# Five edits to the order of loads, splits and products in a conformer, attention and SwiGLU block

## The chip, the cores and the metric

The kernel runs on one core of a Trainium2 chip. The metric is the device time in microseconds (us) of one execution, and the median over several runs is compared. The engines are named as in the profile: PE (the matrix engine, with PEld for its weight loads), DVE (VectorE), ACT (ScalarE), POOL (GpSimd) and SP (SyncE, which only issues transfers). A letter q behind an engine's name (ACTq) marks a DMA issue on that engine's queue.

## What is computed

One block on x of 1024 x 1024 with a conditioning vector c: a token mixer with a convolution branch and an attention branch, merged by sigmoid gates, and a SwiGLU feed-forward part, each between two RMS norms with scale, shift and gate from c.

```python
mod = silu(c) @ ada_w + ada_b
sh1, sc1, ga1, sh2, sc2, ga2 = split(mod, 6)
h = rmsnorm(x, pre_mix_g) * (1 + sc1) + sh1
proj = h @ w_in
glu_in, qkv, gates = split(proj, [1024, 2560])
u = u_val * sigmoid(u_gate)                       # u_val, u_gate = halves of glu_in
u = silu(layernorm(causal_depthwise_conv(u), conv_ln_g, conv_ln_b))
y_conv = u @ w_conv_out                           # 512 -> 1024
y_att = stick_breaking_attention(qkv) @ w_att_out # 512 -> 1024
g_conv, g_att = split(gates, 2)
y = (sigmoid(g_conv) * y_conv + sigmoid(g_att) * y_att) @ w_o
x = x + ga1 * rmsnorm(y, post_mix_g)
h = rmsnorm(x, pre_ffn_g) * (1 + sc2) + sh2
gate, up = split(h @ w_ffn_in, 2)                 # 1024 -> 2 x 2816
y = (silu(gate) * up) @ w_ffn_out
out = x + ga2 * rmsnorm(y, post_ffn_g)
```

All of it is float32.

## The kernel before, in words

Every large product is made of three matmuls: an operand is split into a high part, rounded to the fast format fp32r by an ACT copy (`copy_to`, L145), and a low part, the rest, by a DVE subtraction. The product is high x high, high x low and low x high (in the tables `w[0]` is the high part, `w[1]` the low one). The gates, the feed-forward input and the feed-forward output are besides computed by a scheme of Strassen's kind: of 2 x 2 blocks, seven products instead of eight, whose operands (T1 to T4, s1 to s4) are sums of blocks made on DVE. One product is 12 matmuls of 128 x 512 and fills one PSUM bank.

The stages that the change touches, in order of time:

- **Plain gates and early products, 405 to 466 us.** Two of the 16 gate tiles (`PLAIN`, L617 to L623) are computed directly: ACT makes `sg` by a sigmoid, and `store` (L101) writes it to DRAM from POOL's queue. Then, for seven pairs of gate tiles, `early(i, q)` makes two of the seven products ahead, each into bank `k_i`, which ACT evacuates into `ee` (L635) and stores from its own queue (L636) into `e_d` for q = 0 and `s_d` for q = 1. The `sg` and `ee` tiles share two slots; the `k` banks rotate over three PSUM banks.
- **Gate pairs, layer norm, projection, 466 to 590 us.** `other_five(i)` makes the other five products of a pair; after one of the pairs, `ln_all` does the layer norm of the convolution branch (`cr`, `la`, `lm`; its split outputs are `hhi`, `hlo`, `cb`). `y_conv(n)` then multiplies them by the projection weight `wc` (products `pyc`, L747). `load_w` takes one tile from each of three rotating slot groups: raw, high and low. The high and low slots are the same that the gate pairs' operands (`w_op`) use.
- **Early feed-forward products, 741 to 850 us.** `ke(f, i)` (L1102) makes two of the seven products for feed-forward tiles ahead of the rounds, and `e(f, i)` evacuates them; `wh` and `wlo` make the weight's two parts. `t12`, `t3`, `t4`, `hi_of` and `lo_of` make the operands T1 to T4. `r0` and `r1` are generators: each `next` writes the next step of feed-forward round 0 or 1 (`ffn`, L1372) into the program. This section is written by hand in the order in which it is to run, and `pin` fixes that order on PE, DVE and ACT.
- **Sweep 1, from 1170 us.** `prep1(j, w)` (L1604) splits the weights (`wa11`, `wa12`, through `wop2`, whose slots alternate between the groups `whi` and `wlo`) and the feed-forward's inner activations (`gb11`, `gb21`, through `op2`).

Outside the pinned section a scheduler sorts the instructions of each engine, from the order in which they are written and from priorities; within an engine they then run in that order. A transfer is issued by the engine whose `dma_start` is called, in that engine's order: `load` by SP, `store` by POOL.

## Time and profile before

| | |
|---|---|
| median of 3 runs | 1400.02 us (1399.16 to 1400.69) |
| profiled execution | 1400.8 us, span of its records 1399.0 us |
| granted clock of PE, mean | 0.994 |
| busy share of the span | PE 98%, PEld 82%, DVE 75%, ACT 47%, POOL 8% |
| matmuls | 6778 |

How to read the rows: a timeline row has the start in us from the span's start, the duration, the engine, the line of the kernel, the operation, what it writes and reads, the shape, how many were merged into the row (x), and in brackets the idle time of the engine before it with what ended that idleness. Matmuls overlap, so a row of one has 0.39 us although the next starts 0.23 us later. A row of the waits has the engine, the line, what was waited for, and then us in total, times, longest.

### The profile page before, as it was taken

The page shows a single profiled execution, that of the slowest core. Times are in us where ns is not written, and L with a number is a line of the kernel's source. Part 1 is how long each engine was busy: PE and PEld are TensorE (multiplying, and loading weights), DVE is VectorE, ACT ScalarE, POOL GpSimd, SP SyncE. Part 2 cuts the span into 40 slices and gives each one's busy share as a digit, 9 for nine tenths or more (in the row PEclk, how much of TensorE's full clock was granted, in tenths as well). Part 3 has the DMA queues.
Part 4 walks back from the last instruction along what each step waited for, and adds up shares of the span by engine and source line. Part 5 has one row for each costly group of instructions (what it writes and reads, how often), then busy time and mean ns, then how long its engine had stood idle before and what let it go on. Part 6 is the DMA issues. An engine that isn't in the chain of part 4 may idle for free.

```text
span 1399.0 us, 18714 instructions
## 1 busy us (share of the span) xinstructions
PE 1370.6 (98%) x6778; PEld 1150.3 (82%) x6778; DVE 1043.6 (75%) x1592; ACT 651.5 (47%) x1147; POOL 109.4 (8%) x251
## 2 busy tenths in 40 slices
PE   8999999999999999999999999999999999999996
PEld 5898898998987887888887778888888887888886
DVE  7898586775858789677597887778887876785355
ACT  6375465464546456213366553334454444433441
POOL 0100000000000011000012100001111110000002
PEclk8999999999999999999999999999999999999999
DMA  9512050141359646855845635457777779586736
GB/s 384 204 31 76 31 166 31 61 121 46 123 191 318 203 128 233 308 183 176 311 136 188 196 115 192 142 179 249 252 241 263 248 240 398 176 330 229 249 110 121
DMA packets 94684, 265.01 MB, mean 189 GB/s; under 512 B 10048, under 2 KB 21440, under 8 KB 93568
## 3 DMA queue, kind: packets, MB, share of 16 engines
q1 hardware_dynamic: 74352, 201.68, 43.2%
q0 software_dynamic: 18224, 58.47, 11.9%
q10 hardware_dynamic: 2016, 3.67, 0.7%
q8 instruction: 53, 0.87, 0.3%
q14 instruction: 39, 0.32, 0.1%
HBM read 192.74 MB, written 71.04 MB: 189 GB/s over the span
## 4 chain that ended last, share of the span: by engine, by line
PE 76%; issue 14%; DVE 3%; DMA 3%; ACT 2%; POOL 1%; POOLq 0%; DVEq 0%; SPq 0%; ACTq 0%
PE ka L1001 14%; PE ka L1543 9%; PE kc L1001 8%; PE pwo L919 5%; PE pb L1543 4%; PE pgv L166 3%; PE pyc L747 3%; PE pya L166 3%; PE pv L478 3%; PE pq L166 2%; PE pk L166 2%; PE pgg L166 2%; PE pa L1543 2%; PE kb L1001 2%; PE tr L574 2%
## 5 line engine op out<-in xcount | busy, mean ns | idle before, releaser
L550 ACT ACTIVATE ka<-z 128x128 f32<-128x128 f32 (+2 forms) x96 | 47.4, 496 | 53.0 <-PE z L549 43.7
L556 DVE TENSOR_TENSOR_SCAN ka<-ka,eye 128x128 f32<-128x128 f32 (+1 forms) x64 | 51.9, 824 | 17.1 <-ACT ka L550 17.1
L1543 PE MATMUL ka<-gt,w2f 128*128 128x512 f32 x264 | 63.4, 389 | 0.0
L121 DVE SCALAR_TENSOR_TENSOR ada<-ada,cb 128x1024 f32<-128x1024 f32 x32 | 39.0, 1223 | 27.5 <-DMA ada<-in_ada_dram 27.5
L1543 PEld LDWEIGHTS ka<-gt,w2f 128*128 128x128 f32 x264 | 49.6, 188 | 10.3
L561 DVE TENSOR_TENSOR be<-be,ka 128x127 f32<-128x127 f32 (+2 forms) x96 | 52.0, 553 | 7.2 <-ACT be L552 1.8
L1109 PE MATMUL ke<-b,w_hi 128*128 128x512 f32 x176 | 55.2, 395 | 0.0
L552 ACT ACTIVATE be<-z 128x127 f32<-128x127 f32 (+2 forms) x96 | 47.0, 496 | 3.9 <-PE tr L574 3.8
L574 PE MATMUL tr<-ident,be 128*128 128x128 f32 x288 | 47.3, 272 | 0.0
L559 DVE TENSOR_TENSOR_SCAN ka<-ka 128x512 f32<-128x512 f32 x32 | 40.4, 1274 | 4.3 <-ACT ka L550 4.2
L458 PE MATMUL pcv<-ph,cvw 128*128 128x128 f32 x320 | 43.1, 274 | 0.0
L458 PEld LDWEIGHTS pcv<-ph,cvw 128*128 128x128 f32 x320 | 40.6, 191 | 0.7
L1109 PEld LDWEIGHTS ke<-b,w_hi 128*128 128x128 f32 x176 | 32.9, 188 | 7.9 <-issue 0.7
L580 ACT ACTIVATE ahi<-tr 128x512 fp32r<-128x512 f32 x48 | 28.3, 600 | 23.1 <-PE tr L574 17.4
L145 ACT ACTIVATE gt<-X 128x512 fp32r<-128x512 f32 x33 | 20.3, 629 | 39.6 <-DVE X L1586 17.5
L581 DVE TENSOR_TENSOR alo<-tr,ahi 128x512 fp32r<-128x512 f32 x48 | 32.3, 684 | 8.5 <-ACT ahi L580 8.3
L478 PE MATMUL pv<-wv_hi,hhi 128*128 128x256 f32 x128 | 36.7, 287 | 1.6 <-DVE vst L483 0.9
L145 ACT ACTIVATE s1o<-s 128x512 fp32r<-128x512 f32 x22 | 13.8, 629 | 50.4 <-PE ka L1001 44.0
L574 PEld LDWEIGHTS tr<-ident,be 128*128 128x128 f32 x288 | 34.8, 140 | 2.8
L402 PE MATMUL k<-hhi,a 128*128 128x512 f32 x112 | 35.4, 391 | 1.7 <-ACT ee L635 1.6
L478 PE MATMUL pv<-wv_hi,hlo 128*128 128x256 f32 x128 | 36.7, 287 | 0.0
L478 PE MATMUL pv<-wv_lo,hhi 128*128 128x256 f32 x128 | 36.3, 285 | 0.0
(550 smaller groups left out, 4178.6 us busy)
## 6 DMA issues: line engine op xcount, KB each, us to landing
w_d<-w2o POOLq DMA_DIRECT2D x44, 512.0 KB, 7.5
w2f<-w_d SPq DMA_DIRECT2D x44, 512.0 KB, 4.3
ada<-in_ada_dram SPq DMA_DIRECT2D x32, 512.0 KB, 5.1
w2r<-in_w_dram SPq DMA_DIRECT2D x44, 256.0 KB, 3.8
w1g<-in_w_dram SPq DMA_DIRECT2D x21, 512.0 KB, 3.7
w1u<-in_w_dram SPq DMA_DIRECT2D x21, 512.0 KB, 5.7
cvw<-in_cvw_dram SPq DMA_DIRECT2D x20, 512.0 KB, 3.7
ada_w<-in_ada_dram SPq DMA_DIRECT2D x8, 1024.0 KB, 14.0
```

The source lines that it names most:

```text
L166: pe.matmul(bank, st[:, cols], mv[k][:, c * CH:(c + 1) * CH], start=(i == 0 and s == 0), stop=(i == n - 1 and s == 2))
L458: pe.matmul(cv[:, gi * TM:(gi + 1) * TM], wts[n][:, at:at + P], ph[:, g, SH - 1 - d:SH - 1 - d + TM], start=(d == 0), stop=(d == SH - 1))
L478: pe.matmul(pv[:, :256], st[k][:, tcols], mv[:, wc], start=(k == 0 and i == 0), stop=(k == KT - 1 and i == 2))
L550: act.activation(kap[:, s_lo:s_hi], z[:, zo:zo + w], AF.Sigmoid, bias=0.0, scale=-0.125)
L552: act.activation(beta[:, :m], z[:, zo:zo + m], AF.Sigmoid, bias=0.0, scale=0.125)
L556: dve.tensor_tensor_scan(rev, rev, eye[:, CH - w:][:, ::-1], 0.0, op0=ALU.mult, op1=ALU.add)
L561: dve.tensor_tensor(beta[:, :m], beta[:, :m], kap[:, s_lo + 1:s_lo + 1 + m], op=ALU.mult)
L574: pe.transpose(tr[:, o:o + P], probs[ii][:, jo:jo + P], ident)
L919: pe.matmul(bank_, st[:, cols], mv[k][:, cs], start=(k == 0 and q == 0), stop=(k == KT - 1 and q == 2))
L1001: pe.matmul(bank_, st[:, cols], t[:, mv], start=(first and j == 0 and s == 0), stop=(j == HK - 1 and s == 2), skip_group_check=not first)
L1109: pe.matmul(kbs[f], wes[f][st][:, cols], t[:, mv], start=(i == 0 and j == 0 and q == 0), stop=(j == HK - 1 and q == 2), skip_group_check=i ...
L1543: pe.matmul(dst, w[st][:, cols], g[mv], start=first and s == 0, stop=last and s == 2, skip_group_check=more)
```

## The change

Five edits, in order of the program. No arithmetic is added or removed; four transfers change the queue that issues them.

- A. The stores of the two plain gates are issued by ACT instead of POOL.
- B. The first projection weight (`wc0`) is loaded and split when the pair before the last of the loop has been written, into two tiles of its own in pool `pg`, instead of in `y_conv(0)` in the shared slots.
- C. `ke` runs its eight matmuls with the high part of the weight first, then the four with the low part.
- D. The four `t3` are written ahead of round 0's first step (which splits `s2o`), and the low parts of T3 ahead of the second product of tile 9 and of round 0's second step (which splits `s1o` and `s3o`).
- E. `prep1` creates the two activation operands first, then the two weight operands.

```diff
@@ plain gates
                     act.activation(sg, gb[c], AF.Sigmoid, bias=0.0, scale=1.0)
-                    store(s_d[n][:, c * CH:(c + 1) * CH], sg)
+                    act.dma_start(s_d[n][:, c * CH:(c + 1) * CH], sg)
@@ y_conv
-            if n % 2 == 0:
+            if n % 2 == 0 and n:
                 wcs[n // 2] = load_w(wcv[n // 2], f"wc{n}", act, dve)
@@ the loop over the gate pairs
             other_five(i)
+            if q == len(GPAIRS) - 2:
+                raw = wp.tile([P, T], F32, tag="wraw", name="wc0_raw")
+                load(raw, wcv[0])
+                wcs[0] = [pg.tile([P, T], F32R, name=f"wc0_{nm}") for nm in ("hi", "lo")]
+                copy_to(act, wcs[0][0], raw)
+                dve.tensor_tensor(wcs[0][1], raw, wcs[0][0], op=ALU.subtract)
             if q == LN_AT:
                 ln_all()
@@ ke
-            for j in range(HK):
-                cols = slice(i * CH + j * P, i * CH + (j + 1) * P)
-                t = B[("B11", "B21")[i], j]
-                for q, (st, mv) in enumerate(((0, 0), (0, 1), (1, 0))):
-                    pe.matmul(kbs[f], wes[f][st][:, cols], t[:, mv], start=(i == 0 and j == 0 and q == 0),
-                              stop=(j == HK - 1 and q == 2), skip_group_check=i > 0)
+            for st, mvs in ((0, (0, 1)), (1, (0,))):
+                for j in range(HK):
+                    cols = slice(i * CH + j * P, i * CH + (j + 1) * P)
+                    t = B[("B11", "B21")[i], j]
+                    for mv in mvs:
+                        pe.matmul(kbs[f], wes[f][st][:, cols], t[:, mv],
+                                  start=(i == 0 and j == 0 and st == 0 and mv == 0),
+                                  stop=(j == HK - 1 and st == 1), skip_group_check=i > 0)
@@ the hand-written order
         ke(8, 1)
+        for j in range(HK):
+            t3(j)
         next(r0)
         e(8, 1)
-        for j in range(HK):
-            t3(j)
         ke(10, 0)
         e(10, 0)
+        for j in range(HK):
+            lo_of("T3", j, h2[j, 1])
         ke(9, 1)
         e(9, 1)
         next(r0)
-        for j in range(HK):
-            lo_of("T3", j, h2[j, 1])
@@ prep1
-            return [(wop2(f"wa11_{j}", w[:, 0], act, dve), op2(f"gb11_{j}", x[:, 0], act, dve)),
-                    (wop2(f"wa12_{j}", w[:, 1], act, dve), op2(f"gb21_{j}", x[:, 1], act, dve))]
+            gs = [op2(f"gb{q}1_{j}", x[:, q - 1], act, dve) for q in (1, 2)]
+            return [(wop2(f"wa1{q}_{j}", w[:, q - 1], act, dve), gs[q - 1]) for q in (1, 2)]
```

What the scheduler makes of A on ACT, among the early products: `ee_0` and `ee_1` with the tiles' numbers behind them are the evacuations of the first and second bank, `e_d_0` and `s_d_79` the stores of `early(i, 0)` and `early(i, 1)`, the `a` are weight operands. Rows with a minus stand only in the order before, with a plus only in the new one.

```order
 L635 ACTIVATE ee_0_4227<-k_4211 128x512
+L635 ACTIVATE ee_1_4248<-k_4232 128x512
 L636 DMA e_d_0_95<-ee_0_4227 128x512
+L636 DMA e_d_1_96<-ee_1_4248 128x512
 L145 ACTIVATE T4o_4538<-f_1_4520 128x512
-L635 ACTIVATE ee_1_4248<-k_4232 128x512
-L636 DMA e_d_1_96<-ee_1_4248 128x512
 L145 ACTIVATE a_3_4368<-ew_4308 128x512
```

The second evacuation has moved ahead of the issue of the first one's store, `e_d_0`. Further down, at the evacuation of the second bank's other half:

```order
+L635 ACTIVATE ee_2_4287<-k_4271 128x512
 L636 DMA s_d_79<-ee_0_4266 128x512
-L635 ACTIVATE ee_2_4287<-k_4271 128x512
 L636 DMA e_d_2_97<-ee_2_4287 128x512
 L145 ACTIVATE a_6_4428<-ew_4425 128x512
-L635 ACTIVATE ee_1_4305<-k_4232 128x512
 L145 ACTIVATE T2o_4577<-f_3_4567 128x512
 L145 ACTIVATE T1o_4580<-f_3_4566 128x512
 L145 ACTIVATE T3o_4583<-f_3_4565 128x512
-L636 DMA s_d_81<-ee_1_4305 128x512
+L635 ACTIVATE ee_1_4305<-k_4232 128x512
```

`ee_1_4305` has moved behind three operands of T2, T1 and T3, and `ee_2_4287` ahead of the issue of `s_d_79`.

What it makes of B on ACT, in the layer norm's stretch (tile numbers differ between the two kernels, so a row can stand twice):

```order
 L704 ACTIVATE gw_5116<-gw_5116 128x512
-L145 ACTIVATE s1o_5339<-gs_6_5312 128x512
-L145 ACTIVATE s2o_5319<-gs_6_5313 128x512
+L145 ACTIVATE wc_hi<-wc_raw 128x1024
+L145 ACTIVATE s1o_5345<-gs_6_5318 128x512
+L145 ACTIVATE s2o_5325<-gs_6_5319 128x512
 L704 ACTIVATE gv_5115<-gv_5115 128x512
 L795 ACTIVATE hhi_277<-lm 128x512
 L795 ACTIVATE cb_4978<-lm 128x512
```

The copy of `wc0`'s high part has moved to a place ahead of the last pair's splits `s1o` and `s2o`.

And of E on ACT at the start of sweep 1, in the new order (the `wa` are the weights' high parts, the `gb` the activations'):

```order
L145 ACTIVATE wa_0_10310<-wa_10292 128x512
L1411 ACTIVATE uw_10120<-kc_10118 128x512
L145 ACTIVATE wa_1_10346<-wa_10295 128x512
L145 ACTIVATE wa_1_10349<-wa_10295 128x512
L145 ACTIVATE wa_2_10385<-wa_10298 128x512
L1429 ACTIVATE uw_10120<-uw_10120 128x512
L145 ACTIVATE wa_2_10388<-wa_10298 128x512
L145 ACTIVATE gb_0_10301<-X_10261 128x512
L145 ACTIVATE gb_0_10304<-X_10261 128x512
```

The rows before have the same sequence of `wa` and `gb`; only the tile numbers and lines differ.

## The prediction

> **What bounds the kernel now.** I read the busy times of the page first, then the waits of the matrix engine (PE) over the whole span, then the timelines of the places that those waits name.

> ```profile
> PE 1370.6 (98%) x6778; PEld 1150.3 (82%) x6778; DVE 1043.6 (75%) x1592; ACT 651.5 (47%) x1147; POOL 109.4 (8%) x251
> 850.00:1170.00 320.00, 319.94 (x1412) 264.69 (x1410) 246.22 (x393) 132.64 (x233) 44.60 (x83) 1.00 0.67 232
> PE pyc L747 <- ACT wc_hi L145: 2.1, 1, 2.1
> PE k L402 <- ACT ee L635: 1.6, 1, 1.6
> PE ke L1109 <- DVE w_lo L1043: 1.3, 2, 0.8
> PE ka L1543 <- ACT gb L145: 1.2, 1, 1.2
> ```

> The first row is the page's: PE is busy for 1370.6 of 1399.0 us. The second is one stretch of the table by windows (length, then the busy times of PE, weight loads, DVE, ACT, POOL, then the granted clock): in 320 us of the feed-forward rounds PE idles 0.06 us at full clock. So PE sets the pace, no other engine does, and the 6778 matmuls stay. What can be won is the idle time of PE in the middle of the program, and the last four rows name most of it: who waits, for what, us in total, times, longest. B, A, C and E below aim at one each, 6.2 us together; D aims at two smaller ones that stand in its part. A wait costs more than its row, so I count the loss from one start of a matmul to the next, less the 0.227 us that one advances (319.94 / 1412 of the second row).

> **A, stores of the plain gates on ScalarE's queue.** What stalls PE here:

> ```profile
> 435.81 0.39 PE L402 MATMUL k<-hhi,a 128*128 128x512 f32 x1
> 437.81 0.50 PE L402 MATMUL k<-hhi,a 128*128 128x512 f32 x1 [1.61 <-ACT ee L635]
> 425.26 1.07 POOL L101 DMA_DIRECT2D s_d<-sg  x2 [11.79 <-ACT sg L622]
> 431.79 0.60 ACT L635 ACTIVATE ee<-k 128x512 f32<-128x512 f32 x1 [0.74 <-DMA s_d<-sg]
> 433.52 1.16 ACT L145 ACTIVATE a<-ew 128x512 fp32r<-128x512 f32 x2 [1.13 <-PE k L402]
> 437.18 0.58 ACT L635 ACTIVATE ee<-k 128x512 f32<-128x512 f32 x1
> 437.79 0.33 ACTq L636 DMA_DIRECT2D s_d<-ee  x1
> 441.80 0.60 ACT L635 ACTIVATE ee<-k 128x512 f32<-128x512 f32 x1 [0.31 <-DMA s_d<-ee]
> DMA to landing us min/median/max: 4.1/5.4/6.3
> DMA to landing us min/median/max: 2.0/4.3/6.9
> ```

> PE loses 437.81 − 435.81 − 0.23 = 1.77 us: the sixth early product wants a bank that the evacuation at 437.18 frees. The evacuation at 431.79 did wait for a gate store (0.74 us), which is what the edit shortens. But the one at 437.18 did not: ahead of it stand seven activations, about 0.52 us apart, from 433.52 on, and the first of these waited 1.13 us for a PE product that still read its weight tile. That wait ends at 433.52 whatever the stores do, since PE is no earlier. In the changed order the same seven stand ahead of it, which excludes a gain: 1.77 stays.

> Against it stand two new orders on ACT. First, the issue of e_d_0 now stands behind the second evacuation, hence behind the landing of the second gate store. The last two rows are the landings of the four gate stores from POOL and of the 14 early stores from ACT. By the ACT median, a store issued at about 426.0 (where POOL issued its pair from 425.26 on) lands at 430.3, the evacuation takes its 0.60, the issue of e_d_0 is at about 431.0, and it lands at 435.3, before 437.18 (no loss); with both at 6.9 it lands at about 440.5 (3.3 late). Second, the evacuation of 441.80 now stands behind three activations of T2o, T1o and T3o that followed it; it would end near 443.6 instead of 442.40, and the eighth product wants that bank at 437.81 + 24 × 0.227 = 443.26, so PE waits some 0.4 (the end less 443.26). It also waits for the landing of the store issued at 437.79, which took 441.80 − 437.79 = 4.0; at 6.9 the loss grows by about 1.7 more (2.8 if that issue also slides behind the evacuation now ahead of it). The four more issues on ACT (0.33 each, row of 437.79) lie ahead of the 1.13 us of idleness at 433.52, which hides them; without it two of them would add 0.7 to the chain. A is **+0.4**, from 0 to +3.3, or more if both landings are slow (rival 3).

> [...]

> **B, the first projection weight in own tiles.**

> ```profile
> 552.88 1.52 PE L402 MATMUL kc<-T1o,s1o 128*128 128x512 f32 x6
> 556.46 0.50 PE L747 MATMUL pyc<-hhi,wc_hi 128*128 128x512 f32 x1 [2.06 <-ACT wc_hi L145]
> 533.36 10.70 SPq L98 DMA_DIRECT2D wc_raw<-in_wcv_dram  x2
> 536.70 0.61 ACT L704 ACTIVATE gw<-gw 128x512 f32<-128x512 f32 x1
> 554.31 0.63 ACT L795 ACTIVATE hhi<-lm 128x512 fp32r<-128x512 f32 x1 [1.69 <-DVE lm L793]
> 555.36 1.04 ACT L145 ACTIVATE wc_hi<-wc_raw 128x1024 fp32r<-128x1024 f32 x1
> 538.64 2.14 DVE L793 TENSOR_TENSOR lm<-cr,la 128x1024 f32<-128x1024 f32 x1
> 556.78 1.22 DVE L155 TENSOR_TENSOR wc_lo<-wc_raw,wc_hi 128x1024 fp32r<-128x1024 f32 x1
> 552.13 2.14 DVE L793 TENSOR_TENSOR lm<-cr,la 128x1024 f32<-128x1024 f32 x1 [0.44 <-ACT cr L791]
> ```

> Six matmuls from 552.88 end their turn at 554.24; the next starts at 556.46: 2.22 us lost. The weight's copy ran at 555.36 only because it shares slots with other weights and stands behind layer-norm outputs that waited for DVE. After the change it stands on ACT right behind the gw row of 536.70, its raw tile was issued at 533.36, and by the landings above it is there near 537.7; the copy ends near 538.8, its low part (1.22) follows the lm row on DVE and ends near 541.9. Both are over ten microseconds ahead of 554.24. Six of the projection's matmuls now stand ahead of most of kc's (near 544.3), which puts the end of the six kc rows to 555.6, and nineteen right behind these, so PE has work there; the layer norm's last outputs, made from 554.31 on, are wanted by the fifteenth of the nineteen, at 555.6 + 14 × 0.227 = 558.8. The price: ACT holds 1.04 more near 538 and DVE 1.22 more near 541. DVE's idle gaps up to 552.13, such as that row's 0.44, take it up in part; the layer norm's end may come some 0.8 us later, to about 555.7, which the three microseconds before 558.8 cover. If that cover were gone PE would wait up to 1.2 (the added DVE row whole). B is **−2.2**, from −2.2 to −1.0.

> **C, low parts last in the early feed-forward products.**

> ```profile
> 785.04 0.62 PE L1109 MATMUL ke<-b,w_hi 128*128 128x512 f32 x2
> 786.46 0.50 PE L1109 MATMUL ke<-b,w_lo 128*128 128x512 f32 x1 [0.80 <-DVE w_lo L1043]
> 794.30 0.67 PE L1109 MATMUL ke<-b,w_hi 128*128 128x512 f32 x2
> 795.50 0.50 PE L1109 MATMUL ke<-b,w_lo 128*128 128x512 f32 x1 [0.53 <-DVE w_lo L1043]
> 793.14 1.04 ACT L145 ACTIVATE w_hi<-w_raw 128x1024 fp32r<-128x1024 f32 x1
> 794.21 1.23 DVE L1043 TENSOR_TENSOR w_lo<-w_raw,w_hi 128x1024 fp32r<-128x1024 f32 x1 [1.30 <-ACT w_hi L145]
> ```

> Losses: 786.46 − 785.04 − 0.45 = 0.97 and 795.50 − 794.30 − 0.45 = 0.75. With eight high matmuls (1.82 us) ahead of the first low one, both low parts (the second is done at 795.44, wanted at 796.1) come in time. But the first gain is swallowed: PE would reach the product of 794.30 at 793.33, and its high part is only being made from 793.14 to 794.18, behind high parts that hang on a chain of DVE without a gap. So that product still starts near 794.3. C is **−0.75**, from −0.7 to −1.7 (if the copy too came a microsecond sooner).

> **D, T3's sums ahead of round 0's splits.**

> ```profile
> 801.48 0.69 DVE L992 TENSOR_TENSOR s2o<-s,s2o 128x512 fp32r<-128x512 f32 x1 [2.50 <-ACT s2o L145]
> 802.09 2.73 DVE L1134 SCALAR_TENSOR_TENSOR y<-y,dsh 128x512 f32<-128x512 f32 x4
> 807.40 0.69 DVE L992 TENSOR_TENSOR s1o<-s,s1o 128x512 fp32r<-128x512 f32 x1 [2.58 <-ACT s1o L145]
> 814.64 0.93 PE L1001 MATMUL ka<-T_0o,s3o 128*128 128x512 f32 x3 [0.17 <-DVE uw L1401]
> 821.08 0.93 PE L1001 MATMUL ka<-T_0o,a 128*128 128x512 f32 x3 [0.47 <-DVE uw L1416]
> ```

> The sums (2.73) move into the gap of 2.50, T3's four low parts (four DVE rows of 128x512 like the 0.69 of s1o, some 2.4 in a row) into that of 2.58. So the uw of line 1401 comes about a microsecond sooner and PE does not lose what it lost before 814.64: 0.17 by the row, 0.34 with the 0.17 that the first pause of C cost beyond its row (0.97 against 0.80); but the rest of the chain up to line 1416 moves up by no more than PE does, since four low parts of B22 still stand ahead of it: the loss at 821.08 stays. D is **−0.35**, from 0 to −1.0.

> **E, sweep 1's operands created in another order.**

> ```profile
> 1169.98 0.63 ACT L145 ACTIVATE wa<-wa 128x512 fp32r<-128x512 f32 x1 [1.36 <-PE ka L1001]
> 1170.51 2.70 ACT L145 ACTIVATE gb<-X 128x512 fp32r<-128x512 f32 x5
> 1171.18 1.19 PE L1543 MATMUL ka<-gb,wa 128*128 128x512 f32 x4 [1.24 <-ACT gb L145]
> ```

> PE waits 1.24 for the first gb, which stands behind six wa's, the last of which waited 1.36 for PE to free its slot. The scheduled order of the change has the same six wa's ahead of the first gb on ACT. E is **0**, from 0 to −1.4.

> **Sum.** 0.4 − 2.2 − 0.75 − 0.35 = −2.9. The profiled execution took 1400.8 (span 1399.0), so it becomes 1397.9; the median of the runs is 1400.02, 0.8 below that execution, and the same step gives **1397.1**.

> **Rivals.**
> 1. Every stall that an edit names goes: 1.77 + 2.22 + 1.72 + 0.34 + 0.64 + 1.41 = 8.1 (the last two are 0.47 and 1.24 with 0.17 each), so 1391.9. For it: each edit points at a row of the waits. Against: the activation chain from 433.52, the copy at 793.14 and the unchanged order at 1170 each hold a stall without the edited cause.
> 2. A new wait takes B's place: the projection's first operands are made by the layer norm on the same two engines that now also make the weight, and PE waits there for the low parts instead. For: the 2.14 us lm rows leave DVE gaps of only 0.44. Against: three microseconds of slack. With half or less of B left the time is 1398.3 to 1399.3; I take 1398.9. That the edits do less than they say (A and E nothing, C half) is already in my sum.
> 3. Slower: ACT's queue is in order, so each evacuation that waits for a store's landing holds all issues behind it, and the next landing starts later. Place: the ee rows of 429 to 442. It decides when e_d_0 lands after 437.2 or the store of 437.79 takes over 5 us. With every landing at the 6.9 of the last row there: 0.4 + 3.3 + 2.8 = 6.5 in place of 0.4, so 1403.2. For it: the evacuation of 431.79 waited 0.74 for such a landing. Against: the median of 4.3.

> [...]

> **How the numbers follow.** My forecast has 0.55, with its own range 1395.5 to 1398.7; rival 1 has 0.10, rival 2 0.25, rival 3 0.10 (over its lighter forms too, most of them between 1398.5 and 1402.8). The forecast is likeliest at **1397.1**. The range of 8 in 10, **1394.0 to 1400.4**, holds the forecast, rival 2 and the lighter half of rival 3, and reaches from partial successes of A, C and E on the low side to A at its upper bound on the other. A measurement of this kernel can tell 0.2%, 2.8 us, from no change, that is a time below 1397.2 or above 1402.8. The forecast lies on that edge: 0.36 of its 0.55 faster, 0.19 the same. With rival 1 **faster is 0.46**; with rival 2 and most of rival 3 **the same is 0.48**; **slower is 0.06**.

> **What would show it.** Right: no wait of pyc for wc_hi and PE without a gap near 554; one ke row left that waits, now for ACT's w_hi near 794, none for w_lo; the row of uw L1401 gone, that of L1416 still there; the gb row of sweep 1 as before; the k row for ee still there at 1.6, a small second one near 443. Wrong: a new wait of pyc for hlo or cb (rival 2), waits of k for ee over 3 us in all (rival 3), or k's wait gone (the chain from 433.52 was not the cause).

## The result, and the profile after

| | before | after |
|---|---|---|
| median of the runs, us | 1400.02 (7 runs, 1398.91 to 1405.62) | 1395.44 (7 runs, 1394.56 to 1396.38) |
| profiled execution, us (span) | 1400.8 (1399.0) | 1395.44 (1393.4) |
| mean granted clock of the profiled execution | 0.994 | 0.994 |
| PE busy, us (matmuls) | 1370.6 (6778) | 1368.1 (6778) |

The ratio is 0.9962, with a 95% interval of 0.995 to 0.9973, that is 3.8 to 7.0 us; the medians differ by 4.6 us. That is faster, by more than the 0.2% that can be told from no change. The forecast was 1397.1 with a range of 1394.0 to 1400.4: the time lies inside, 1.7 us below the forecast and 0.06 below the forecast's own range of 1395.5 to 1398.7. On the direction the chances leaned, by 0.48 to 0.46, to "the same", and it came out faster. One execution of the kernel before, beside the experiments, took 1718.0 us at a granted clock of 0.75; it is left out of all that follows.

The waits of PE in the profile after (engine and line, what it waited for, us in total, times, longest):

```profile
PE k L402 <- ACT ee L635: 1.6, 1, 1.6
...
PE ka L1551 <- ACT gb L145: 1.2, 1, 1.2
PE ke L1116 <- ACT w_hi L145: 1.1, 1, 1.1
...
PE ka L1007 <- DVE uw L1424: 0.5, 1, 0.5
PE ka L402 <- DVE s2o L389: 0.4, 1, 0.4
```

Against the rows of before, the wait of pyc for the projection's weight is gone, the two waits of ke for w_lo have become one for w_hi, and the earlier of the two uw rows is gone. The waits of k for ee, at which A was aimed, and of ka for gb, at which E was, are as long as they were.

The same places in PE's timeline after (start, us, engine, operation, tiles, the idle time before it and what ended it):

```profile
436.34 0.50 PE L402 MATMUL k<-hhi,a 128*128 128x512 f32 x1 [1.61 <-ACT ee L635]
...
552.43 1.75 PE L402 MATMUL kc<-T1o,s1o 128*128 128x512 f32 x7
554.01 0.61 PE L747 MATMUL pyc<-cb,wc_hi 128*128 128x512 f32 x2
...
787.57 1.07 PE L1116 MATMUL ke<-b,w_lo 128*128 128x512 f32 x4
789.71 2.11 PE L1116 MATMUL ke<-b,w_hi 128*128 128x512 f32 x8 [1.07 <-ACT w_hi L145]
791.66 1.07 PE L1116 MATMUL ke<-b,w_lo 128*128 128x512 f32 x4
...
815.17 0.94 PE L1007 MATMUL ka<-T_0o,a 128*128 128x512 f32 x3 [0.46 <-DVE uw L1424]
...
1165.25 1.20 PE L1551 MATMUL ka<-gb,wa 128*128 128x512 f32 x4 [1.24 <-ACT gb L145]
```

The seven kc matmuls from 552.43 (7 × 0.227 = 1.6 us) last until 554.01, and the projection's matmul starts at that very moment: nothing is left of the 2.22 us. The products of ke now come as eight matmuls with w_hi and four with w_lo; only the one at 789.71 waits, for the high part.

**Where the 4.6 us lie.** Both kernels issue the same number of matmuls, and outside the stretches that the edits reorder the i-th matmul of one is the i-th of the other. So I took the start of the i-th matmul after the change less the start of the i-th before, each counted from its own kernel's first matmul, and looked where this shift changes:

| us in the trace of before | shift there, us | step, us | what lies in it |
|---|---|---|---|
| up to 424 | −1.12 | −1.12 | no edit: 0.93 of it is one wait of pq for wq_hi at 306 |
| 430 | −1.48 | −0.36 | A: a weight load's wait at 425 |
| 446 | −1.14 | +0.34 | A: the pause before the eighth early product |
| 527 | −1.60 | −0.46 | no edit: PE's wait for s2o |
| 565 | −3.94 | −2.34 | B |
| 735 | −4.12 | −0.18 | no edit, in small pieces |
| 760 | −4.54 | −0.42 | no edit: two small pauses of psq have become one |
| 800 | −5.34 | −0.80 | C |
| 823 | −5.90 | −0.56 | D |
| 1300 | −5.93 | −0.03 | E |

The step at 430 is small and easy to count as chance, but it goes with A. There a weight load of the early products waits 0.5 us behind ACT's `sg` row at line 622, and ahead of that ACT and DVE wait for a load of `f`. The wait of the weight load before, then DVE's wait before and after:

```profile
PEld k L402 <- ACT sg L622: 0.5, 1, 0.5
419.46 0.69 DVE L685 TENSOR_TENSOR f<-f 128x512 f32<-128x512 f32 x1 [5.67 <-DMA f<-xm_d]
417.81 0.69 DVE L685 TENSOR_TENSOR f<-f 128x512 f32<-128x512 f32 x1 [5.12 <-DMA f<-xm_d]
```

All five profiles with the gate stores on POOL's queue have such a wait of the weight load, of 0.3 to 0.5, and none of the nine with the stores on ACT's. DVE's wait is 5.45 to 5.67 us in those five and 4.98 to 5.23 in the nine. Why that load lands sooner no run shows. In the other four profiles with POOL's queue the shift falls there too, by 0.02 to 0.20 against before, so I put 0.16 to 0.34 of the 0.36 down to A.

The edits account for −0.36 + 0.34 − 2.34 − 0.80 − 0.56 = **−3.7**, the places without an edit for −2.2 more in this pair of profiles. The wait of pq at 306 is in the profile of before alone, not in the other thirteen, so that part is chance. How much of the rest is chance is the question that the medians leave; it is taken up behind the experiments.

### The profile page after: what moved, and what is told of

It reads as the page before. It is cut to its first block, busy times and chain, and to the rows that moved or that the text cites. A ratio compares the mean times of both kernels' runs of the same rounds, so it can differ in the third digit from the quotient of the medians.

```text
span 1393.4 us, 18713 instructions
## 1 busy us (share of the span) xinstructions
PE 1368.1 (98%) x6778; PEld 1150.9 (83%) x6778; DVE 1043.6 (75%) x1592; ACT 651.4 (47%) x1147; POOL 107.1 (8%) x247
## 4 chain that ended last, share of the span: by engine, by line
PE 89%; DVE 6%; ACT 2%; issue 1%; DMA 1%; SPq 0%; DVEq 0%; ACTq 0%
PE ka L1007 15%; PE ka L1551 9%; PE kc L1007 8%; PE pwo L925 6%; PE pb L1551 4%; PE ke L1116 4%; PE pgv L166 3%; PE pya L166 3%; PE pyc L747 3%; PE pv L478 3%; PE pcv L458 3%; PE k L402 2%; PE pq L166 2%; PE pk L166 2%; PE pgg L166 2%; PE ka L402 2%
## 5 line engine op out<-in xcount | busy, mean ns | idle before, releaser
L1116 PE MATMUL ke<-b,w_hi 128*128 128x512 f32 x176 | 44.5, 395 | 1.1 <-ACT w_hi L145 1.1
L145 ACT ACTIVATE gt<-X 128x512 fp32r<-128x512 f32 x33 | 20.3, 629 | 38.3 <-DVE X L1594 13.9
L145 ACT ACTIVATE s1o<-s 128x512 fp32r<-128x512 f32 x22 | 13.8, 629 | 50.6 <-PE ka L1007 44.2
L402 PE MATMUL k<-hhi,a 128*128 128x512 f32 x112 | 35.4, 391 | 1.7 <-ACT ee L635 1.6
```

The costliest lines, as they stand in the source:

```text
L402: pe.matmul(bank_, w[st][:, cols], mvs[mv], start=(first and j == 0 and s == 0), stop=(j == HK - 1 and s == 2), skip_group_check=not first)
L1116: pe.matmul(kbs[f], wes[f][st][:, cols], t[:, mv], start=(i == 0 and j == 0 and st == 0 and mv == 0), stop=(j == HK - 1 and st == 1), skip ...
```

## The experiments

"Pause" means here, as in the expectations, the time from the start of a matmul to the start of the next; a matmul without a pause has 0.227 us. All experiments keep the computation whole. Times are medians; the kernel before ran on the same chip beside each.

| kernel | us (runs) | before beside it, us | ratio, 95% interval |
|---|---|---|---|
| all edits but A | 1395.62 (10) | 1401.02 | 0.9969, 0.9956 to 0.9983 |
| before + B | 1396.95 (10) | 1401.02 | 0.9971, 0.9959 to 0.9983 |
| before + C and D | 1399.80 (10) | 1401.02 | 0.9997, 0.9981 to 1.0012 |
| the change + third slot | 1393.57 (4) | 1401.02 | 0.9949, 0.9931 to 0.9968 |
| the change again | 1395.27 (10) | 1401.88 | 0.9955, 0.9942 to 0.9967 |
| the change + w_hi earlier | 1394.55 (1) | 1401.88 | one execution |
| the change + gb first | 1398.44 (1) | 1401.88 | one execution |
| all three additions | 1392.68 (4) | 1401.88 | 0.9935, 0.9912 to 0.9959 |
| the same, gb first in part | 1391.71 (4) | 1401.04 | 0.9932, 0.9905 to 0.9958 |
| before + third slot | 1402.26 (1) | 1401.04 | one execution |
| before + A | 1400.92 (1) | 1401.04 | one execution |
| the change + w_hi made four times | 1401.04 (10) | 1400.26 | 1.0006, 0.9996 to 1.0015 |

### All edits but A

```diff
 # the change
-                    act.dma_start(s_d[n][:, c * CH:(c + 1) * CH], sg)
+                    store(s_d[n][:, c * CH:(c + 1) * CH], sg)
```

> All edits but A: the plain gates' stores go back to POOL's queue. My theory: A itself wins nothing at the early products (the 2.00 us from start to start near 436 stays in both) and costs one small pause of PE near 442 (0.44 from start to start, 0.21 lost); whatever it costs is taken back at the wait for s2o near 526, whose length follows from when PE arrives there. So without A the small pause is gone, the s2o pause is longer by about the same, and the time is that of the full change within 0.5 us (1395.0 to 1396.0). Rival, A is worth its own half microsecond because the faster stores bring the layer norm's stretch forward: without A the time is 0.5 us or more above the full change and the s2o pause back at its 1.2 us of before without PE arriving any earlier. Second rival, A is a loss that stays: 0.3 us or more below the full change.

Waits of PE in this kernel:

```profile
PE k L402 <- ACT ee L635: 1.6, 1, 1.6
...
PE ke L1116 <- ACT w_hi L145: 1.1, 1, 1.1
...
PE ka L402 <- DVE s2o L389: 0.4, 1, 0.4
```

The first pause of k is 2.00 with and without A; the small one before the eighth product, 0.44 in the change, is not there in this kernel. So A costs 0.21 at that pause, 0.34 by the shift around it. It wins 0.26 at the weight load near 425, so over the stretch from 400 to 446 us the change comes out only 0.08 us slower than the kernel without A. The medians differ by 0.2 us between 1395.62 and 1395.44, which no interval here can tell. The s2o pause stayed at 0.78, as in the full change: it neither took A's loss back nor went back to the 1.23 of before, so it is not A that moves it.

### B alone

```diff
 # before
-            if n % 2 == 0:
+            if n % 2 == 0 and n:
                 wcs[n // 2] = load_w(wcv[n // 2], f"wc{n}", act, dve)
 ...
+            if q == len(GPAIRS) - 2:
+                raw = wp.tile([P, T], F32, tag="wraw", name="wc0_raw")
+                (the load, its two own tiles, the copy and the low part as in the change)
```

> The kernel before with edit B alone (first projection weight early, in own tiles). My theory: B carries half of the result. The pause of 2.4 us from start to start ahead of pyc goes to 0.23, nothing else moves: 2.2 to 2.4 us below the kernel before (ratio 0.9983 or so), the pauses of the early feed-forward products (1.18 and 0.93) and of the round-0 product (0.56) as before. Rival, the gain is mixed with others: a new pause for hlo or cb, or the pauses at psq near 743 change with B (they were 0.54 and 0.53 before, one of 0.44 after), which would make B worth 2.6 to 2.9.

Waits of PE:

```profile
PE ke L1115 <- DVE w_lo L1049: 1.4, 2, 0.8
...
PE ka L402 <- DVE s2o L389: 0.8, 1, 0.8
...
PE ka L1007 <- DVE uw L1407: 0.2, 1, 0.2
```

The pyc row is gone and the others stand as before. At the median this is 4.1 us under the kernel before beside it, with an interval of 2.4 to 5.7 worked out from the ratio's, where the place lost 2.3. B is thus the larger part of the change, and it seems worth more than its pause. Up to the s2o pause of 526 us the instructions of DVE, ACT, SP and POOL have the same order here and in the kernel without A, word for word, yet that pause was 1.22 here and 0.78 there. Part of the 4.1 is a matter of which executions were compared: among those with a mean clock of 0.994 alone, B's six have a median of 1396.4 and the seven of the kernel before beside them 1399.1, 2.7 apart.

### C and D alone

```diff
 # before: ke's loops and the hand-written order as in the change, nothing else
```

> The kernel before with edits C and D alone. My theory: the first of the two low-part pauses goes but returns as a wait for w_hi of the next tile (1.4 to 1.5 from start to start), the second goes, the pause before the T3 product of round 0 goes, that before its T4 product (0.85) stays: 0.75 + 0.35 to 0.5 = 1.1 to 1.25 us below the kernel before. Rival, all that the two edits name is won: 1.72 + 0.33 + 0.62 = 2.7 us below. Rival, nothing, since the chain of DVE behind the early products sets the end of the section: 0 to 0.3.

At their places both did what was expected: one pause of 1.45 for w_hi, none for w_lo, no T3 pause, 0.84 before the row that waits for uw; the shift falls by 0.80 and 0.57 there. But the time moved by only 1.2 us, inside its uncertainty. The profiled execution, of 1401.7, shows why it says little. Waits of PE:

```profile
PE ka L402 <- DVE s2o L389: 2.1, 1, 2.1
PE pyc L747 <- ACT wc_hi L145: 2.1, 1, 2.1
PE k L402 <- ACT ee L635: 2.0, 2, 1.8
...
PE ke L1110 <- ACT w_hi L145: 1.1, 1, 1.1
```

The s2o pause, at which neither edit works, is 2.49 us instead of 1.23. The k row counts two waits although A is not in this kernel: the store issued at 436.39 took 5.34 us to land, ACT waited 1.01 for it with an evacuation, and the pause before the eighth product is 0.65. And behind the wait for wc_hi something else happens. PE's timeline, and three windows (length, then busy us of PE, weight loads, DVE, ACT and POOL with their instructions, then the granted clock, the DMA share and GB/s):

```profile
556.96 0.50 PE L747 MATMUL pyc<-hhi,wc_hi 128*128 128x512 f32 x1 [2.06 <-ACT wc_hi L145]
...
558.56 0.63 PE L747 MATMUL pyc<-cb,wc_hi 128*128 128x512 f32 x1
558.99 0.63 PE L747 MATMUL pyc<-hlo,wc_hi 128*128 128x512 f32 x1
```

```profile
555.00:558.00 3.00, 1.04 (x4) 0.91 (x5) 2.82 (x5) 2.43 (x4) 0.28 (x1) 0.97 1.02 419
558.00:561.00 3.00, 3.00 (x8) 2.32 (x8) 1.10 (x2) 0.00 (x0) 0.26 (x1) 0.50 1.03 421
561.00:564.00 3.00, 3.00 (x14) 2.42 (x14) 0.56 (x1) 0.57 (x1) 0.00 (x0) 0.96 1.03 414
```

The matmuls behind the wait start 558.99 − 558.56 = 0.43 us apart instead of 0.227, and in the 3 us from 558 the granted clock is 0.50. Seven intervals are so, 7 × 0.2 = 1.4 us. The same wait of 2.06 in the profile of before had no such stretch.

### What stalls the early products

If the wait of k for ee is not the gate stores' queue, it may be the two slots that gate tiles, evacuations and stores share. One kernel gives the tag a third slot in the change, with half of one block of cb moved into it to make room; one gives it to the kernel before; one puts A alone on the kernel before.

```diff
 # the change + third slot (and, with the first lines alone, before + third slot)
-  tag="sg", ... bufs=2
+  tag="sg", ... bufs=3
-  back = pg.tile([P, 2, CH], F32R, tag="cb", name=f"cb{ct}", bufs=1)
-  back = [back[:, q] for q in range(2)]
+  back = [sgp.tile([P, CH], F32R, tag="sg", name=f"cb{ct}0", bufs=3),
+          pg.tile([P, CH], F32R, tag="cb", name=f"cb{ct}1", bufs=1)]
 # before + A
-                    store(s_d[n][:, c * CH:(c + 1) * CH], sg)
+                    act.dma_start(s_d[n][:, c * CH:(c + 1) * CH], sg)
```

> The full change with a third slot for the tiles that gates and early products share (one half of a layer-norm output moves into the third slot to make room). With it no evacuation there waits for a store that has just been issued, and the scheduler puts the evacuation that frees the first bank ahead of the seven activations. My theory: the pause of 2.00 us near 436 is a matter of that order and goes nearly whole, 1.5 to 1.8 us below the full change, provided that the layer norm's stretch follows PE. Rival, the stretch near 520 is set by DVE and loads alone: then the pause for s2o near 526 grows by what is won and the time is that of the full change within 0.4 us. Rival, the pause near 436 is set by the weight operands and stays.

> The kernel before, with its gate stores on POOL's queue, and a third slot for the tiles that gates and early products share. My theory: which queue issues the gates' stores has no part in the pause of 2.00 us before the sixth early product, only the two shared slots have: it goes to 0.23 here as it did with the stores on ACT, and the pause of 2.4 ahead of pyc and those of 1.18 and 0.93 in the early feed-forward products stay. Rival: with the stores on POOL some of the 2.00 stays.

> The kernel before with edit A alone. My theory: the pause of 2.00 us before the sixth early product stays and the small one before the eighth comes up (0.4 to 0.9 from start to start), all others as before: 0.2 to 0.6 us lost. Rival, faster stores do bring something: the first pause below 1.8.

Waits of PE in the kernel before with a third slot, its stores still on POOL's queue:

```profile
PE pyc L747 <- ACT wc_hi L145: 2.1, 1, 2.1
PE pvar L250 <- ACT sq L247: 1.9, 2, 1.3
PE ke L1109 <- DVE w_lo L1043: 1.4, 2, 0.8
```

The row of k is gone, in the change with a third slot too: both pauses, 2.00 and 0.44, are away, the shift against the change falls by 2.25 there, and 1393.57 is 1.9 under the change. With A alone on the kernel before, the 2.00 stays and the 0.44 appears. So the slots, with the order that the scheduler makes of them, hold the stall, and the queue does not: the gate stores landed within 4.2 to 6.2 us in the first of these kernels (POOL's queue) and 2.4 to 5.0 in the second (ScalarE's), and the stall was away in both.

The single times of the two kernels built on before are not to be compared. The first of them had a slow start of the program, which is told of below, and seven matmuls at half clock behind the wait of pyc; the second had an s2o pause of 2.36 us with seven matmuls at half clock behind it. Half of what the second lost there came back: its pause of pyc, which ends with a copy on ACT, was 1.17 instead of 2.44. Its expectation, all other pauses as before, did not hold.

### The copy of w_hi that C waits for

```diff
 # the change
+        wh(9)
         for j in (0, 1): hi_of("T1", j, h2[j, 0])
-        wh(9)
```

> The full change with the high part of tile 9's weight written ahead of the first two high parts of T1. My theory (the second half of edit C's gain hangs on that copy): the pause of 1.45 from start to start for w_hi falls to 0.4 or less, 1.0 us below the full change, and the low part then comes in time behind the eight high matmuls. Rival, the pieces of T1 that now come a microsecond later hold the round-0 products, and the time is the same. Rival, the copy waits for its slot, and the pause stays.

The prediction said that C's first pause is swallowed because the next product waits for its high part, behind high parts of other operands on ACT. Here that copy goes ahead of two of them. PE and ACT in this kernel:

```profile
787.69 1.07 PE L1116 MATMUL ke<-b,w_lo 128*128 128x512 f32 x4
788.79 2.11 PE L1116 MATMUL ke<-b,w_hi 128*128 128x512 f32 x8
```

```profile
787.69 1.04 ACT L145 ACTIVATE w_hi<-w_raw 128x1024 fp32r<-128x1024 f32 x1
```

The copy starts at 787.69 (788.62 in the change) and the product follows the last one by 788.79 − 787.69 = 1.10, where four matmuls take 0.91, instead of 2.14. One microsecond comes back at the place, the one that C had lost there. In this execution the pause before the eighth early product was 0.86 instead of 0.44, since the store issued at 435.98 took 5.35 us to land (4.77 in the change), so the single time shows 0.9 and not 1.0.

### Sweep 1's first operands

E did nothing, since the scheduled order on ACT had not changed. Here the order is forced: the weights of the second and third pair are issued behind the first gb's.

```diff
 # the change, prep1
+            if j in (1, 2):            # in the last kernel of this group: if j == 2
+                with tc.issue_after(gb0[1].ins):
+                    ws = [wop2(f"wa1{q}_{j}", w[:, q - 1], act, dve) for q in (1, 2)]
```

> The full change with an order constraint on ACT: the weight operands of sweep 1's second and third tile behind the first tile's two activation operands. My theory (edit E did nothing because the scheduler kept the six weight operands ahead of the first activation operand): the pause of 1.24 us for gb ahead of sweep 1 goes, 1.2 to 1.4 us below the full change, no new pause for wa in the sweep. Rival, the inner activations themselves are loaded too late: the pause stays. Rival, the second weight operands then come late and the pause moves behind the first eight matmuls.

The pause went from 1.63 to 0.49, and a new one of 1.15 came 22 us later. ACT and PE there:

```profile
1187.86 0.63 ACT L145 ACTIVATE wa<-wa 128x512 fp32r<-128x512 f32 x1 [11.30 <-DMA wa<-in_w_dram]
```

```profile
1190.48 1.88 PE L1551 MATMUL ka<-gb,wa 128*128 128x512 f32 x7 [0.76 <-DVE gb L1537]
```

ACT waited 11.30 us for the load of a weight tile; DVE made its low part behind that, and the low part of the gb that PE waits for behind this. The weight's load could be issued only when its slot was freed, which the constraint had made later, so it stood behind the loads of X and Y on SP's queue. The gain was given back by that: 1.14 won, 0.92 lost. The next two kernels hold this constraint and the two edits above; in the second it is put on j = 2 alone.

> The full change with the third slot, the order constraint of sweep 1 and the earlier copy of tile 9's weight together. My theory (each pause of PE in the middle of the program is worth its length and they add up): 1.98 + 1.4 + 1.0 = 4.4 us below the full change, about 1391 us. Rival, what is won at the early products is lost again where a chain of DVE sets the pace: 2.5 us below or less.

> As the kernel with all three mends (third slot, earlier copy of tile 9's weight, order constraint in sweep 1), but only the weight operands of the third tile stand behind the first activation operands, those of the second do not. My theory: the pause of 1.2 us that came up twelve microseconds into the sweep was a load of a weight tile (fifth of the sweep) that fell behind two other loads on SP's queue because the second tile's operands, whose slot it takes, were made later; now that load keeps its place, and 1.1 us more is won: 3.9 us below the full change, about 1391.4 us. Rival, the pause is set by DVE's work in the first microseconds of the sweep (twelve low parts and eight sums): it stays, and the time is 2.7 us below the full change.

The first of them missed its expectation: 1392.68 is 2.8 us under the change and not 4.4, with a late pause of 1.21 in sweep 1. SP's queue in it, with the constraint on both pairs:

```profile
1165.91 1.12 SPq L98 DMA_DIRECT2D X<-g_d  x1
...
1170.51 14.30 SPq L98 DMA_DIRECT2D wa<-in_w_dram  x4
```

and in the second, with its waits of PE:

```profile
1167.43 1.10 SPq L98 DMA_DIRECT2D wa<-in_w_dram  x1
...
1170.23 0.52 SPq L98 DMA_DIRECT2D X<-g_d  x1
```

```profile
PE ka L402 <- DVE s2o L389: 0.8, 1, 0.8
...
PE ka L1007 <- DVE uw L1424: 0.5, 1, 0.5
```

In the second the weight's load is ahead of X again, as in the change, and neither the early nor the late pause of sweep 1 is there; k, ke and gb have no row among the waits shown first. Its median of **1391.71** is 3.7 us under the change's 1395.44 and 0.68% under the kernel before (0.9932, 0.9905 to 0.9958): the lowest median of this study, though with four runs its interval overlaps that of the change again (0.9942 to 0.9967). The rival, that DVE's own work sets the late pause, falls with it: ahead of that pause, with gb first, DVE sat idle for 7.83 us.

### A longer pause on purpose

The half-clock stretch of C and D alone, and of the two kernels built on before, came behind waits of PE of 2.0 to 2.1 us, but not behind every such wait. To see whether it belongs to the wait, the copy that C waits for is made four times.

```diff
 # the change
-            copy_to(act, hi, raws[key])
+            for _ in range(4 if key == 9 else 1):
+                copy_to(act, hi, raws[key])
```

> The full change with the high part of tile 9's weight copied four times instead of once, so that PE's pause for it in the early feed-forward products grows from 1.45 us (start to start) by three copies of 0.95 to 1.04 us, to 4.3 to 4.6. In three of the five pauses of 2.0 us or more for DVE or ACT in the middle of the program, in the profiles so far, the granted clock fell to half for the three microseconds behind the pause (seven or eight matmuls 0.43 apart instead of 0.23, 1.5 us more); it did so behind none of 1.6 us. My theory: a pause over about two microseconds costs more than its length, so here the next 7 to 16 matmuls run 0.43 apart and the early products end 1.5 us or more later than the pause alone makes them: 4.4 to 5 us above the full change. Rival: the slow matmuls of those profiles belonged to the place at 556 or to the run; here all matmuls behind the pause are 0.23 apart and the loss is the 2.9 to 3.1 us of the three copies.

PE's timeline and two windows:

```profile
787.95 1.07 PE L1117 MATMUL ke<-b,w_lo 128*128 128x512 f32 x4
793.34 3.08 PE L1117 MATMUL ke<-b,w_hi 128*128 128x512 f32 x8 [4.32 <-ACT w_hi L145]
796.22 1.73 PE L1117 MATMUL ke<-b,w_lo 128*128 128x512 f32 x4
```

```profile
794.00:797.00 3.00, 3.00 (x9) 2.35 (x8) 3.00 (x6) 2.25 (x4) 1.00 (x2) 0.53 0.62 175
...
800.00:803.00 3.00, 3.00 (x15) 2.49 (x14) 1.78 (x4) 2.35 (x5) 0.30 (x1) 1.00 0.61 243
```

Three more copies took 3.3 us more of waiting (the pause grew from 1.45 to 4.71), and behind it seven matmuls run 0.43 us apart at a clock of 0.53. The shift at the place against the change is 4.8 us, inside the expectation of 4.4 to 5; the medians differ by 5.8 (1401.04 against 1395.27), which is outside it. The s2o pause, 1.20 here and 0.78 there, is 0.4 of that. Seven of the ten executions have a mean clock of 0.991 and the profiled one 0.993, so most may have had more than one slow stretch; no profile shows it. In the profile, this wait cost its own length and some 1.4 us after it.

### The change again

> The full change once more, as the base of this group of runs. Between 1394.5 and 1396.5 us, the pauses of PE (from start to start) as in its first profile: 2.00 before the sixth early product, 0.44 before the eighth, 1.45 for w_hi in the early feed-forward products, 0.85 before the T4 product of round 0. The pause for s2o near 526, which was 0.8 to 2.5 in the five profiles so far without an edit there, tells whether it belongs to a kernel or to a run: to a kernel if it is 0.77 again.

In this second profile the pauses were 2.00 and 0.44 for k, 0.78 for s2o, 1.44 for w_hi and 0.89 for uw, where the first had 2.00, 0.44, 0.77, 1.46 and 0.85; the time was 1395.27 over ten runs, on another chip. The result is the change's own.

## Why the prediction was right, and where not

**What bounds the kernel.** Right. PE set the pace, the matmuls stayed 6778, and every step of the time is a step of a PE pause.

**A: right at the early products, with a term missing.** Forecast +0.4, measured +0.34 there: the 1.77 us stayed, the small wait near 443 came. But the forecast put what A does ahead of the early products at nothing, and the weight load's wait at 425 went with it, −0.36 in this pair. So A as a whole comes to about 0, at the lower end of its range. The step "that wait ends at 433.52 whatever the stores do" held for the queue, as A alone and all but A show. But the order of ACT ahead of the stall is not given by PE alone: with a third slot, on either queue, the scheduler made another order and the stall was gone. The text took the order for a fact of the program where it was a consequence of two shared slots.

**B: right at its place, too small in time.** Forecast −2.2, measured −2.34, and rival 2 did not come: pyc waited for neither hlo nor cb. What the term lacked is the clock behind the wait. Three profiles have this wait of 2.06 us, and in two of them (C and D alone, and the kernel before with a third slot) the next seven intervals ran at half clock; in the third, that of before, they did not. So in part of the executions the wait had cost 1.4 us more than its length, and B removed that too; the last section works out how often, 0.6 to 0.8 us in the mean of the executions by an estimate. The profile that the forecast was made from could not show it.

**C: right.** Forecast −0.75, measured −0.80. The first pause was swallowed by the wait for w_hi, as the text said, and putting that copy earlier gave the microsecond.

**D: right in kind.** Forecast −0.35, measured −0.56: the row of uw at line 1401 is gone, that of 1416 (now 1424) stands. The row is 0.33 of it, as forecast; the other 0.2 lie in small pieces that no row names.

**E: right.** Forecast 0, measured −0.03: the order that decides did not move. The forced order won 1.1 us there only when the load on SP's queue kept its place.

**Rival 1** (every stall goes) fell on the three stalls that the prediction had kept: k's, w_hi's, gb's. All three were removed afterwards, by other means than these edits. **Rival 3** (the landings hold ACT's queue) did not come. Its point of decision was e_d_0 landing after 437.2 or a store over 5 us; the order was as it said, but the first two e_d stores landed in time, the store in the place of that of 437.79 took 4.77, and the 7.0 of one evacuation's store shows in no wait of PE. In two other profiles its second condition was met: that store took 5.34 us (C and D alone) and 5.35 (w_hi earlier), and the pause before the eighth product was 0.65 and 0.86. So the mechanism exists, at 0.4 us in two of fourteen profiles, not at the 6.5 of the rival. Landings after the change, of the gate stores and then of the evacuations' stores:

```profile
DMA to landing us min/median/max: 2.4/4.5/4.9
DMA to landing us min/median/max: 2.0/4.5/7.0
```

The median of the gate stores was 5.4 before, from POOL's queue, and is 4.5 now, from ACT's; no wait of PE in these two profiles ends with the landing of a gate store.

**The sum: −2.9 was too small.** At the places of the edits the steps make −3.7, 0.8 more than the forecast: A 0.42, D 0.21, B 0.14, C 0.05. The medians differ by 4.6. The remaining 0.9 are not at the edits. The executions by their mean granted clock:

| mean clock of the execution | before: runs, median us | after: runs, median us |
|---|---|---|
| 0.994 | 15, 1399.31 | 7, 1395.43 |
| 0.993 | 13, 1400.76 | 9, 1395.18 |
| 0.992 | 13, 1401.51 | none |
| 0.989 to 0.991 | 16, 1402.39 to 1405.92 | 1, 1399.09 |

(After: the 7 runs of the result and the 10 of the repetition. Before: the 57 executions that ran beside the experiments.) Between executions of 0.994 the difference is 3.9 us, 0.7 less than between the medians. From 0.994 to 0.993 the kernel before loses 1.45 us, about what seven matmuls at half clock cost, and the kernel after loses nothing; this fits the wait of pyc, which only one of them has, though most of these executions have no profile. The mean clock alone does not show a slow stretch, since it also takes in the half clock at the end of the program (from 1392.4 us on in the profile of before, from 1387.2 in that of the change): the second profile of the change has 0.993 and no slow stretch in its middle. Executions of 0.989 to 0.991 are 16 of 57 before and 1 of 17 after; the slower start of the program, told of below, is one way to such a mean, and its share moves a median too.

**Left open** are 0.2 to 0.4 us of the 3.9, by how much of the step at 430 is A's. Two pauses that no edit touches were shorter after the change. That of s2o was 0.77 or 0.78 in seven of the fourteen profiles, the change and the kernel before with a third slot among them, and 0.93 to 2.49 in the other seven, before and the fastest kernel among them. Ahead of it stands a DVE row that waits for a load, here in the profile after:

```profile
517.27 0.69 DVE L713 TENSOR_TENSOR gs<-gw5b 128x512 f32<-128x512 f32 x1 [2.69 <-DMA gw5b<-in_win_dram]
```

This wait was 3.58 and 3.70 us in the two profiles with a pause over 2.3, and 2.24 to 2.84 in the other twelve, so the two long pauses follow that load; the step from 0.78 to 1.2 does not show in it.

The pause of psq near 743 was double in six profiles and single in the others. Whether the change makes either likelier, these runs don't say.

## What to carry to other kernels

A pause of the engine that sets the pace is not always worth its own length (here a wait of 2.06 us was followed by 1.4 us more in two profiles of three): look at the interval of the matmuls and at the granted clock behind it, and in more than one profile. An edit can also work at a place that nobody aimed it at, as A did at 425: compare the whole shift of the matmuls, not only the rows that it names. When a stall waits for an evacuation, ask which slots the scheduler had to order it by before looking at the queue of a store; and when an order is forced, look at the loads whose issue hangs on the slots that it frees later. An edit that is said to reorder something costs nothing to judge: for E the rows of the scheduled order were the same, and the shift at its place was −0.03 us.

## What the runs showed of the hardware

**The clock dropped behind some waits of about two microseconds, and not behind all.** Over all profiles of this study, in the part from 430 us on: behind 17 pauses of 1.44 to 1.63 us and 10 of 1.99 to 2.16, no matmul was slower. Behind five of 2.36 to 2.49, three were followed by seven intervals of 0.43 us and two were not. Behind the one of 4.71 it was so.

| profile and wait of PE | step of the grid, us | PE idle in it, us | clock in the next step |
|---|---|---|---|
| before, pyc 2.06 | 552.76 to 556.17 | 1.77 | 1.00 |
| C and D alone, s2o 2.1, in two steps | 523.68 to 527.10 and 527.10 to 530.51 | 0.92 and 1.17 | 1.00 |
| C and D alone, pyc 2.06 | 554.40 to 557.82 | 2.06 | 0.50 |
| before + third slot, pyc 2.06 | 553.57 to 556.98 | 2.06 | 0.50 |
| before + A, s2o 2.0 | 524.28 to 527.70 | 1.96 | 0.50 |
| w_hi made four times, 4.32 | 787.36 to 790.77 | 1.75 | 1.00 |
| the same wait | 790.77 to 794.18 | 2.57 | 0.50 |

So in the middle of the program these profiles part by how much of a wait fell into one step of the grid: 1.96 us or more was followed by half clock, 1.77 or less never, in any of them. Cut so, the equal waits of 2.06 us differ, 1.77 of it in one step in the profile of before and all of it in the other two, and the wait of 1.6 to 1.8 before the sixth early product never cost more than its length. A sharp limit is not shown: at the end of the program steps with 1.93 and 1.98 us of idleness kept the full clock. By an estimate from these numbers, a wait of 2.06 us at a random place on the grid leaves 1.96 us or more in one step in (3.41 − 2.06 + 2 × 0.10) / 3.41 = 0.45 of the executions, and 1.77 or more in 0.57; at 1.4 us each, the wait of pyc cost 0.6 to 0.8 us beyond its length in the mean.

**The start of the program had a faster and a slower form.** In two of the profiles, the change with gb first and the kernel before with a third slot, the half clock near the start lasted six steps of the grid, 20.48 us (from 20.9 and 21.1 on), instead of the three steps, 10.24 us, of the other twelve. They are 3.3 and 3.8 us behind the change at 100 us, ahead of every edit. In the step before the half clock near the start PE was idle for 0.35 us in the first profile of the change and for 1.07 in that of before, less than the 1.96 us or more ahead of those in the middle; what sets it and its length no run shows. The first 100 us of the change:

```profile
0.00:100.00 100.00, 91.16 (x492) 74.85 (x493) 80.16 (x126) 55.27 (x91) 7.68 (x32) 0.95 0.55 216
```

and of the change with gb first:

```profile
0.00:100.00 100.00, 92.14 (x468) 75.66 (x469) 76.91 (x120) 52.18 (x85) 7.68 (x32) 0.90 0.55 216
```

At a granted clock of 0.90 instead of 0.95, 24 matmuls fewer are done in these 100 us. Single executions of these kernels are therefore no measure of an edit worth a microsecond; the starts of matmuls around the edit are.
